# Head norm of a hybrid decoder layer: eight row pieces at a time, or the whole tile with repeated operands

## Chip, cores and metric

One core of a Trainium2 chip runs the whole layer. The metric is device time in microseconds. A profiled execution gives the rows of the trace; its span is counted from the first to the last instruction.

## The reference

One decoder layer on 1024 tokens of width 1024, in float32. Half of the mixing width is multi-scale retention (4 heads of 128), the other half is RWKV-7 time mixing (8 heads of 64). Both read one normalised input projection; their outputs go through one output projection, a SwiGLU feed-forward part and a gated per-layer embedding, and a last RMS norm closes the layer. The part that matters here is the end of the RWKV-7 half, where the output of each head is normalised over its 64 elements:

```python
def head_norm(y, eps):
    mu = jnp.mean(y, axis=-1, keepdims=True)
    var = jnp.mean(jnp.square(y - mu), axis=-1, keepdims=True)
    return (y - mu) * lax.rsqrt(var + eps)

y = head_norm(y, RWKV_GN_EPS).reshape(B, S, W) * ln_w + ln_b
bonus = jnp.sum(r * k * r_k, axis=-1, keepdims=True) * v
return (y + bonus.reshape(B, S, W)) * g
```

## The kernel before

The large products (input projection, output projection, feed-forward) run on TensorE as a stream of 128x512 matmuls. Each float32 weight is loaded, split into a high and a low part (`split`, L249: the high part on ScalarE, the low part at L251 on VectorE or GpSimd), and multiplied in three passes. This stream is the generator `dense`, and its matmuls are the tile `d` of the trace.

The RWKV-7 half is done by `rwkv_group(p, hf)`, once for each pair of heads `p` (four) and each half `hf` of the sequence (two): eight groups. A group goes through the stages prep, ops, A, tok, mid, chain and fin. Stage A holds the inverse of a triangular matrix by 31 steps of two small VectorE operations (L649 to L652, tiles `tmp` and `R`), each of which needs the one before. The inverse of one group runs while an earlier group is in its later stages.

`weave` (L128) gives out the program: it takes a step of the oldest group that may go on, or else a step of a side task (retention, low-rank parts, loads of the mixed output), or else a step of the dense stream. It counts TensorE's estimated time, and each `yield` of a group says how much of it must pass before the next step (FINW, 8049 ns, between the head norm and the transposes behind it, times a factor of 1.58 or 1.98). The order in which an engine finally takes its instructions is planned when the kernel is built, from the order in which they were given out, priorities and estimated costs.

In stage fin the output of a group lies as 128x512 in `Y`, channels down the partitions. TensorE transposes it in four blocks into the PSUM tile `py`, so that tokens lie down the partitions and the row holds eight pieces of 64 elements, one for each head and block. L778 and L779 take mean and variance of each piece into `mv`, L781 the reciprocal root into `rs` (eight values for each partition), both slices of the small tile `fs`. L784 then subtracts the mean and multiplies by the root, one piece at a time, into `yn`. TensorE transposes `yn` back into `pyt`, which takes the same PSUM buffer as `py`, and L789 to L791 apply gain, bias, bonus and gate and write the result out for the output projection.

Of the kernel before, what the change touches and what calls it, by code (L numbers as in the profile page):

```python
# [12 lines left out]
ALU = mybir.AluOpType  # L13
# [3 lines left out]
P = 128  # L17
# [6 lines left out]
C = 64  # L24
# [154 lines left out]
def tile_hybrid_layer(ctx: ExitStack, tc: tile.TileContext, I, out):  # L179
# [3 lines left out]
    V = nc.vector  # L183
# [31 lines left out]
    def K(n):  # L215
        return cst[:, _C[n][0]:_C[n][1]]
# [136 lines left out]
    with ExitStack() as s1:  # L353
# [194 lines left out]
        def v3(t):  # L548
            return t.rearrange("p (u t) -> p u t", t=C)
# [6 lines left out]
        def rwkv_group(p, hf):  # L556
# [9 lines left out]
            def tf(name):  # L566
                return t2.tile([P, HS], F32, tag="f", name=name, bufs=HBUF)
# [63 lines left out]
            for g in range(2):  # L631
# [5 lines left out]
                for j in range(2):  # L637
                    V.tensor_tensor(out=d0v[:, j, us, :], in0=pbv[:, :, 0, j * 32:(j + 1) * 32],
                                    in1=K(f"ms{j}").unsqueeze(1).broadcast_to([P, 4, 32]), op=ALU.mult)
# [5 lines left out]
                            in1=d0v[:, 1].rearrange("p u t -> p t u").unsqueeze(2).broadcast_to([P, 32, 4, NU]), op=ALU.add)  # L645
# [3 lines left out]
            for i in range(31, 0, -1):  # L649
                V.tensor_tensor(out=tmp[:, :, 0:i], in0=Dt[:, i:i + 1, 0:i].broadcast_to([P, 8, i]),  # L650
                                in1=R[:, :, i:i + 1].broadcast_to([P, 8, i]), op=ALU.mult)
# [31 lines left out]
            for src, dst in ((aak, lambda h: XR[:, :, 1, :]), (v3(v), lambda h: Vbd[:, :, h, :]), (bk[:, 0], lambda h: BA[:, :, 0, :]),  # L683
# [5 lines left out]
                for j, h in ((0, 0), (1, 1), (0, 1), (1, 0)):  # L689
# [4 lines left out]
                            in1=K("nblk").unsqueeze(1).unsqueeze(3).broadcast_to([P, NU, 4, 32]), op=ALU.mult)  # L694
# [75 lines left out]
            py = psr.tile([P, 512], F32, tag="rm", name="py")  # L770
# [4 lines left out]
            mv = fs[:, 48:64].rearrange("p (i c) -> p i c", i=8)  # L775
            va, rs, nw = fs[:, 64:72], fs[:, 72:80], fs[:, 80:88]
# [3 lines left out]
            V.tensor_scalar(out=va, in0=mv[:, :, 1], scalar1=64e-5, scalar2=None, op0=ALU.add)  # L780
            rsqrt(rs, va, nw)  # L781
            yn = tf("yn")
            for i in range(8):
                V.tensor_scalar(out=yn[:, i * C:(i + 1) * C], in0=py[:, i * C:(i + 1) * C], scalar1=mv[:, i, 0:1], scalar2=rs[:, i:i + 1], op0=ALU.subtract, op1=ALU.mult)  # L784
            yield "fin", FINW
            pb = psr.tile([P, 512], F32, tag="rm", name="pyt")
            for i in range(4):
# [149 lines left out]
        for o in order:  # L937
            i = int(o[1])
# [363 lines left out]
        for h in range(2):  # L1302
            for k in range(KT):
                tasks[f"mix{h}{k}"] = (mix_load(h, k), 0, ["wo0" if h else "x0free", f"ret{k}{h}" if k < 4 else f"group{k - 4}{h}"])
        weave([(f"group{p}{hf}", rwkv_group(p, hf), need[p]) for hf in range(2) for p in range(4)],
              tasks, dg, count, pe, done)

# [142 lines left out]
    for a, b in passes:  # L1450
        h, n = a // HS, b - a
        t = slice(a - h * HS, b - h * HS)
        for d in range(KT):
# [10 lines left out]
            i = 0  # L1464
# [85 lines left out]
```

## Time and profile before

| | |
|---|---|
| median of 3 runs | 1594.36 us |
| the runs | 1588.4, 1594.36 and 1594.75 us |
| profiled execution | 1588.42 us, its span 1586.6 us |
| mean granted TensorE clock | 0.988 of full speed |
| TensorE busy | 1490.3 us |
| VectorE busy | 1210.2 us |

Busy time of an engine is the time in which at least one of its instructions runs; two that overlap are counted once. PE is TensorE, PEld its weight loads, DVE VectorE, ACT ScalarE and POOL GpSimd.

### The profile page before, as it was taken

How to read it: one execution, taken by the hardware profiler on the slowest of the kernel's cores; microseconds unless marked ns; L12 is line 12 of the kernel's file. 1: busy time of each engine (PE TensorE's matmuls, PEld its weight loads, DVE VectorE, ACT ScalarE, POOL GpSimd, SP SyncE). 2: the span in 40 equal slices, each digit the busy share in tenths (PEclk: the TensorE clock that was granted, in tenths of full speed). 3: DMA queues.
4: the chain of work that ended last, by engine and by line, in shares of the span. 5: the costliest groups of instructions: out<-in, count | busy, mean ns of one | idle time of the engine just before them, and what ended most of it. 6: DMA issues, size and time to landing. Idle time of an engine off the chain costs nothing.

```text
span 1586.6 us, 21684 instructions
## 1 busy us (share of the span) xinstructions
PE 1490.3 (94%) x7328; PEld 1218.7 (77%) x7328; DVE 1210.2 (76%) x2466; ACT 719.9 (45%) x1442; POOL 516.1 (33%) x389
## 2 busy tenths in 40 slices
PE   6999899998988899978889999999999999999997
PEld 5777778786777677767678877778888888888897
DVE  7668896969799878893965545768888888886675
ACT  6655444434535556344344324543333333334554
POOL 7411111111222124324234340545555555570000
PEclk9999999999999999999999999999999999999998
DMA  6544242343634556343243536332223222331222
GB/s 203 173 159 163 96 131 85 102 141 94 197 115 148 185 175 195 93 126 118 84 132 110 179 120 191 117 114 91 89 87 93 90 90 88 119 93 56 84 87 80
DMA packets 108767, 194.09 MB, mean 122 GB/s; under 512 B 12272, under 2 KB 16496, under 8 KB 108656
## 3 DMA queue, kind: packets, MB, share of 16 engines
q1 hardware_dynamic: 108656, 192.71, 38.3%
q8 instruction: 58, 0.95, 0.2%
q14 instruction: 53, 0.43, 0.1%
HBM read 151.24 MB, written 41.42 MB: 121 GB/s over the span
## 4 chain that ended last, share of the span: by engine, by line
PE 63%; DVE 23%; DMA 5%; ACT 4%; issue 3%; POOL 2%; SPq 0%; DVEq 0%; ACTq 0%; POOLq 0%
PE d L190 36%; PE pd L190 14%; PE pg L190 6%; DVE tmp L650 3%; DVE R L652 3%; POOL lo L251 1%; DVE lo L251 1%; DVE Dm L644 1%; DVE inv L603 1%; PE pb L190 1%; DMA st<-in_w_up_dram 1%; DMA st<-in_w_gate_dram 1%; ACT hi L250 1%; PE pq L196 1%; PE pkh L190 1%
## 5 line engine op out<-in xcount | busy, mean ns | idle before, releaser
L190 PE MATMUL d<-hT,hi 128*128 128x512 f32 x1408 | 449.6, 400 | 6.8 <-ACT hi L250 6.8
L251 POOL TENSOR_TENSOR lo<-st,hi 128x512 fp32r<-128x512 f32 x173 | 244.6, 1415 | 571.6 <-ACT hi L250 456.7
L190 PE MATMUL d<-x,hi 128*128 128x512 f32 x960 | 320.4, 409 | 8.3 <-ACT x L339 7.5
L190 PEld LDWEIGHTS d<-hT,hi 128*128 128x128 f32 x1408 | 263.0, 191 | 59.1 <-ACT hi L250 9.2
L190 PE MATMUL d<-hT,lo 128*128 128x512 f32 x704 | 279.6, 397 | 9.8 <-POOL lo L251 4.9
L250 ACT ACTIVATE hi<-st 128x512 fp32r<-128x512 f32 x298 | 186.7, 627 | 222.1 <-PE d L190 70.5
L190 PE MATMUL pd<-ring 128*128 128x512 f32 x948 | 260.4, 389 | 0.0
L190 PEld LDWEIGHTS d<-x,hi 128*128 128x128 f32 x960 | 176.7, 192 | 42.6 <-ACT x L339 7.5
L190 PEld LDWEIGHTS pd<-ring 128*128 128x128 f32 x948 | 178.0, 188 | 37.0
L190 PE MATMUL d<-x,lo 128*128 128x512 f32 x480 | 192.9, 402 | 3.1 <-POOL lo L251 3.1
L190 PEld LDWEIGHTS d<-hT,lo 128*128 128x128 f32 x704 | 134.1, 190 | 42.1 <-DVE lo L251 7.5
L251 DVE TENSOR_TENSOR lo<-st,hi 128x512 fp32r<-128x512 f32 x125 | 117.4, 949 | 51.8 <-ACT hi L250 50.3
L1152 DVE TENSOR_TENSOR x<-x,pd 128x512 f32<-128x512 f32 x180 | 118.5, 679 | 26.9 <-PE pd L190 26.9
L251 POOL TENSOR_TENSOR ring<-xr,ring 128x512 fp32r<-128x512 f32 x53 | 73.4, 1389 | 146.1 <-ACT ring L250 67.1
L250 ACT ACTIVATE ring<-rm 128x512 fp32r<-128x512 f32 x87 | 53.8, 629 | 131.5 <-DVE rm L1085 84.6
L190 PEld LDWEIGHTS d<-x,lo 128*128 128x128 f32 x480 | 91.9, 192 | 23.4 <-POOL lo L251 5.2
L652 DVE TENSOR_TENSOR R<-R,tmp 128x248 f32<-128x248 f32 (+30 forms) x248 | 87.4, 352 | 3.7
L650 DVE TENSOR_TENSOR tmp<-Dt,R 128x248 f32<-128x248 f32 (+30 forms) x248 | 84.2, 339 | 3.4
L190 PE MATMUL d<-mix,hi 128*128 128x512 f32 x256 | 80.7, 395 | 0.9 <-ACT hi L250 0.9
L251 DVE TENSOR_TENSOR ring<-rm,ring 128x512 fp32r<-128x512 f32 x65 | 61.3, 946 | 12.5 <-ACT ring L250 11.6
L250 ACT ACTIVATE ring<-xr 128x512 fp32r<-128x512 f32 x57 | 34.9, 625 | 74.2 <-PE pd L190 73.2
L190 PEld LDWEIGHTS d<-mix,hi 128*128 128x128 f32 x256 | 47.3, 189 | 10.5 <-ACT hi L250 1.3
(315 smaller groups left out, 2389.3 us busy)
## 6 DMA issues: line engine op xcount, KB each, us to landing
st<-in_w_gate_dram SPq DMA_DIRECT2D x88, 256.0 KB, 2.9
st<-in_w_up_dram SPq DMA_DIRECT2D x88, 256.0 KB, 2.9
st<-in_w_in_dram SPq DMA_DIRECT2D x86, 256.0 KB, 2.9
xr<-in_w_down_dram SPq DMA_DIRECT2D x44, 256.0 KB, 2.9
retd<-rt SPq DMA_DIRECT2D x32, 256.0 KB, 2.8
rr<-retd SPq DMA_DIRECT2D x32, 256.0 KB, 3.2
st<-in_w_o_dram SPq DMA_DIRECT2D x32, 256.0 KB, 3.0
rkvd<-rkvt SPq DMA_DIRECT2D x24, 256.0 KB, 2.1
```

Of the source, the lines that this page charges most:

```text
L190: m = nc.tensor.matmul(ps, lhsT, rhs, start=start, stop=stop, skip_group_check=more)
L196: return nc.tensor.transpose(ps, x, ident)
L250: act(hi, src, AF.Copy)
L251: return (eng or V).tensor_tensor(out=lo, in0=src, in1=hi.bitcast(F32), op=ALU.subtract)
L603: V.reciprocal(out=inv, in_=inv)
L644: V.tensor_tensor(out=Dm, in0=d0v[:, 0].rearrange("p u t -> p t u").unsqueeze(2).broadcast_to([P, 32, 4, NU]), in1=d0v[:, 1].rearrange("p ...
L650: V.tensor_tensor(out=tmp[:, :, 0:i], in0=Dt[:, i:i + 1, 0:i].broadcast_to([P, 8, i]), in1=R[:, :, i:i + 1].broadcast_to([P, 8, i]), op=AL ...
L652: V.tensor_tensor(out=R[:, :, 0:i], in0=R[:, :, 0:i], in1=tmp[:, :, 0:i], op=ALU.subtract)
L1152: V.tensor_tensor(out=dst, in0=dst, in1=ps, op=ALU.subtract if name == "P4" else ALU.add)
```

## The change

The eight operations of L784, each on 128x64 with the piece's mean and root as one value for each partition, become two operations on the whole 128x512 tile, seen as 128x8x64. The first subtracts the eight means, the second multiplies by the eight roots in place; mean and root are operands that are repeated along the last axis.

```diff
             yn = tf("yn")
-            for i in range(8):
-                V.tensor_scalar(out=yn[:, i * C:(i + 1) * C], in0=py[:, i * C:(i + 1) * C], scalar1=mv[:, i, 0:1], scalar2=rs[:, i:i + 1], op0=ALU.subtract, op1=ALU.mult)
+            for src, m, op in ((py, mv[:, :, 0:1], ALU.subtract), (yn, rs.unsqueeze(2), ALU.mult)):
+                V.tensor_tensor(out=v3(yn), in0=v3(src), in1=m.broadcast_to([P, 8, C]), op=op)
             yield "fin", FINW
```

`v3` (L548) views a 128x512 tile as 128x8x64.

## Rows read from the trace of the kernel before

**Rows 1.** The page's head: span, and each engine's busy time.
```profile
span 1586.6 us, 21684 instructions
...
PE 1490.3 (94%) x7328; PEld 1218.7 (77%) x7328; DVE 1210.2 (76%) x2466; ACT 719.9 (45%) x1442; POOL 516.1 (33%) x389
```
**Rows 2.** The page's chain that ended last, by engine.
```profile
PE 63%; DVE 23%; DMA 5%; ACT 4%; issue 3%; POOL 2%; SPq 0%; DVEq 0%; ACTq 0%; POOLq 0%
```
**Rows 3.** The changed line's instructions: ns min/median/max, first and last start.
```profile
L784 DVE TENSOR_SCALAR yn<-py,fs x64: 330/339/351, 223.4 to 895.1; 128x64 f32<-128x64 f32 x64
```
**Rows 4.** Chain in order of time, third and sixth group: start us, us, what.
```profile
390.47 0.25 DVE yn L784
...
392.92 0.26 DVE yn L784
...
681.94 0.26 DVE yn L784
...
684.36 0.25 DVE yn L784
```
**Rows 5.** Timeline of VectorE, second group: start us, us, instruction.
```profile
308.97 0.34 DVE L784 TENSOR_SCALAR yn<-py,fs 128x64 f32<-128x64 f32 x1
...
311.67 0.17 DVE L650 TENSOR_TENSOR tmp<-Dt,R 128x8 f32<-128x8 f32 x1
311.75 0.68 DVE L455 TENSOR_TENSOR rt<-d,R 128x512 f32<-128x512 f32 x1
312.35 1.11 DVE L652 TENSOR_TENSOR R<-R,tmp 128x8 f32<-128x8 f32 x1
```
**Rows 6.** Timeline of VectorE, end of the inverse beside the first group.
```profile
227.17 0.18 DVE L650 TENSOR_TENSOR tmp<-Dt,R 128x8 f32<-128x8 f32 x1
227.38 0.18 DVE L652 TENSOR_TENSOR R<-R,tmp 128x8 f32<-128x8 f32 x1
227.59 0.45 DVE L654 STREAM_TRANSPOSE tmp<-R 128x256 f32<-128x256 f32 x1
```
**Rows 7.** Timeline of VectorE, fifth group (eight merged into one row).
```profile
578.18 2.10 DVE L784 TENSOR_SCALAR yn<-py,fs 128x64 f32<-128x64 f32 x8
580.20 0.74 DVE L340 SCALAR_TENSOR_TENSOR hT<-rr,par,hT 128x512 fp32r<-128x512 f32 x1
```
**Rows 8.** Instructions of three lines with two tensor operands, as in rows 3.
```profile
L840 DVE TENSOR_TENSOR rr<-rsc,rmisc x8: 678/682/693, 262.3 to 907.3; 128x512 f32<-128x512 f32 x8
...
L825 DVE TENSOR_TENSOR rr<-rr x16: 628/684/1778, 187.0 to 858.8; 128x512 f32<-128x512 f32 x16
...
L644 DVE TENSOR_TENSOR Dm<-d x8: 2236/2270/2330, 124.0 to 759.4; 128x1024 f32<-128x1024 f32 x8
```
**Rows 9.** Groups of instructions, 200 to 910 us: busy us, mean ns.
```profile
L825 DVE TENSOR_TENSOR rr<-rr 128x512 f32<-128x512 f32 x15 | 12.3, 822 | 0.0
```
**Rows 10.** The page's costliest groups: the two operations of an inverse step.
```profile
L652 DVE TENSOR_TENSOR R<-R,tmp 128x248 f32<-128x248 f32 (+30 forms) x248 | 87.4, 352 | 3.7
L650 DVE TENSOR_TENSOR tmp<-Dt,R 128x248 f32<-128x248 f32 (+30 forms) x248 | 84.2, 339 | 3.4
```
**Rows 11.** Fourth group: the changed line, and the transposes behind it.
```profile
L784 DVE TENSOR_SCALAR yn<-py,fs x8: 336/337/340, 486.3 to 490.6; 128x64 f32<-128x64 f32 x8
...
L196 PEld LDWEIGHTS pyt<-cst,yn x4: 140/140/143, 491.0 to 491.3; 128*128 128x128 f32 x4
```
**Rows 12.** Busy time by stretch: us, then PE, PEld, DVE, ACT, POOL, granted clock, DMA share, GB/s.
```profile
680.00:690.00 10.00, 9.25 (x51) 7.88 (x52) 10.00 (x44) 6.49 (x16) 2.65 (x3) 1.00 0.50 159
...
700.00:710.00 10.00, 6.96 (x35) 5.88 (x35) 8.66 (x10) 5.63 (x16) 1.28 (x1) 0.83 0.74 222
710.00:720.00 10.00, 8.13 (x35) 6.38 (x36) 8.95 (x12) 6.19 (x13) 5.19 (x3) 0.83 0.36 109
720.00:730.00 10.00, 7.90 (x33) 5.59 (x31) 2.08 (x3) 5.27 (x12) 3.53 (x4) 1.00 0.42 131
730.00:740.00 10.00, 9.17 (x33) 7.42 (x34) 2.07 (x3) 2.29 (x4) 3.30 (x3) 0.83 0.43 131
```

## The prediction, made before the change was run

> **What bounds the kernel now.** I read the page's head first, then its chain, then the busy shares by stretch, then the rows of the line that is changed. TensorE is busy 1490.3 of 1586.6 us and VectorE 1210.2 [rows 1], and the chain that ended last runs 63% of the span on TensorE and 23% on VectorE [rows 2]. So a shorter VectorE queue is worth something only where the chain is on VectorE at that moment. The line that is changed runs in eight places, from 223.4 to 895.1 us, once for each pair of heads and each half of the sequence, eight operations each: 64 of them, 339 ns in the median and never outside 330 to 351 ns [rows 3]. What runs after the last of them is untouched, except for the moment at which it starts.
>
> The chain in order of time passes through these operations in two of the eight places: third group, 390.47 to 393.17 us, and sixth group, 681.94 to 684.61 us, each time through all eight [rows 4] (the first and the last of eight). In the other six the chain is on TensorE, ScalarE, GpSimd or a load while they run. That is the first cut: six of eight savings have no direct way to the end of the kernel.
>
> **What is removed.** By busy time the eight operations cost 8 x 0.339 = 2.71 us a group. That is not what they cost the queue. The code gives out the 62 operations of the triangular inverse (L649 to L652) in one piece, yet on the queue they alternate with L784 [rows 5], so the queue's order is planned when the kernel is built. And it is a good fit: the inverse is a chain in which each operation needs the one before it, and an independent operation in between starts before its predecessor has ended. From 308.97 to 311.75 us eight L784 and eight inverse steps go by in 2.78 us [rows 5]. Inverse steps of this width alone stand 0.21 us apart [rows 6], eight take 1.7 us. So the eight L784 lengthen the queue there by 2.78 - 1.7 = 1.1 us, not by 2.71. Six groups (first to fourth, sixth, seventh) alternate like this; in the fifth and eighth the eight stand alone and take 580.20 - 578.18 = 2.02 us [rows 7].
>
> **What is added.** Two operations of 128x512. The first reads PSUM and one small SBUF operand, repeated along the row; its nearest row is L840, PSUM with a repeated SBUF operand, 682 ns with 693 at most [rows 8]. The second reads SBUF twice, in place; nearest is L825, 684 ns in the median but 1778 at most [rows 8] and 822 in the mean over this stretch [rows 9]. A repeated operand as such is free here: L650 has one repeated along the last axis and L652 none, and at equal width they take 339 and 352 ns [rows 10]. The worst stride in the trace is L644, 2270 ns for 1024 elements [rows 8], or 1.14 us for 512; I take 0.68 and keep 1.14 as the bound, since the repeat lies in the operand's last axis as in L650.
>
> In the queue a 512-wide operation between two inverse steps puts them 312.35 - 311.67 = 0.68 us apart instead of 0.21 [rows 5], so it adds 0.47; two add 0.94. An interleaved group thus gains 1.1 - 0.94 = 0.15 us. Alone, the two need 0.68 + 0.03 + 0.60 = 1.31 us (the second waits for the first, the only wait that is added, and the operation queued behind it starts some 0.08 early): gain 2.02 - 1.31 = 0.71 us in the fifth and eighth, where the chain doesn't pass. If other work fills every gap, the eight cost 2.02 and the two 1.20: gain 0.82, the upper end. On the chain the sum is therefore 2 x 0.15 = 0.3 us up to 2 x 0.82 = 1.6 us; the rows with inverse steps between are the nearest, and I take 0.7.
>
> [...]
>
> **The port.** L784 reads PSUM and was not once stretched [rows 3]; the new second operation has two SBUF inputs, the kind that is sometimes stretched to 1.78 us [rows 8]. The mean extra of L825 is 822 - 684 = 0.14 us [rows 9], so 0.28 us in the two places on the chain and 1.1 us in all eight. Taken off the 0.7, the direct effect is -0.4 us. [...]
>
> **What else moves.** The PSUM tile of the transposed heads is freed when its last reader ends: one operation instead of eight, some 2 us sooner. Its next user of note, the transposes back, are put later in TensorE's order by FINW; in the tightest place the last L784 starts at 490.6 and the transposes at 491.0 us [rows 11], right behind other matmuls, so nothing waits there now and nothing is gained. It also shows the thin cover: in the fourth group a second operation stretched by 1.1 us would stand in front of TensorE for about 0.8 us.
>
> **The sum.** Profiled execution: 1588.42 - 0.4 = 1588.0 us. The median of the runs is 5.94 us above the profiled execution (two of the three runs lie there), so the likeliest time is 1594.36 - 0.4, that is 1594.0 us. No change can be told under about 0.5%, 8 us.
>
> **Rivals.**
> *The saving goes through whole (faster).* If VectorE's queue sets the pace in all eight places, the groups give back their busy time: 64 x 0.339 - 16 x 0.685 = 10.7 us, less the mean stretch of 1.1: 1594.4 - 9.6 = 1584.8 us. For it: VectorE is busy all of 680 to 690 us [rows 12], with the chain on it. Against it: the chain touches L784 in two places only, and the interleaving hides over half. With what a shifted plan can give on top I hold this case at 0.26.
>
> *The queue is planned anew for the worse (slower).* Forty-eight operations fewer and sixteen longer ones change the order in which VectorE's ready work is taken, and the long ones cannot be slipped between inverse steps in small change. If a weight split (L251) falls behind, TensorE runs dry. [...] Against it: VectorE is only relieved. Chance 0.16.
>
> *The port takes it back (slower).* Should the second operation meet a GpSimd operation in all eight places, it costs 8 x (1.78 - 0.68) = 8.8 us: 1594.0 + 8.8 = 1602.8 us. It decides only if at least seven of eight collide and each is on the way to the end; the mean of L825 says about two in fifteen (15 x 0.14 / 1.1). Chance 0.06.
>
> **The numbers.** Forecast, within 0.5%: 0.52. Faster 0.26, slower 0.16 + 0.06 = 0.22. The range must hold both the 1584.8 of the one side, with some room for a luckier plan, and the 1601.8 to 1606.9 of the other: 1580 to 1607 us. The forecast's own range is 1586 to 1602.
>
> **What would show it.** In the changed kernel's trace: sixteen operations of about 0.68 us on the changed lines, the first always near 0.68, the second now and then 1.1 to 1.8; VectorE's busy time down by some 10 us while the span hardly moves; inverse steps no longer paired, 0.21 us apart, in the stretch where L784 stood; the chain still on TensorE and loads around 223, 309, 487, 579, 801 and 894 us. I am wrong if the chain leaves VectorE at 390 and 682 us over a microsecond sooner, if TensorE's idle time in 400 to 800 us changes by more than 8 us, or if the order of the splits and loads far from these groups has changed.

## The result: slower by 0.9%, and the profile after

The changed kernel takes 1604.35 us (median of 6 runs, 1597.93 to 1608.65), the kernel before 1588.47 us beside it (6 runs, 1584.71 to 1594.75). The ratio over all runs is 1.0086, with a 95% interval of 1.0069 to 1.0104; the quotient of the two medians, 1.0100, lies within it. I had forecast no change that can be told, with slower at 0.22. The time lies inside the stated range, near its upper end, and that by luck: the upper end was counted from 1594.0 us, where the kernel before has a median of 1588.47, and counted from there it would lie below the time measured.

The page's head of the changed kernel, which answers to [rows 1]:

```profile
span 1603.3 us, 21623 instructions
...
PE 1496.9 (93%) x7328; PEld 1222.3 (76%) x7328; DVE 1204.4 (75%) x2418; ACT 721.0 (45%) x1442; POOL 519.0 (32%) x389
```

VectorE has 48 instructions fewer and is busy 5.8 us less, and the span is 16.7 us longer. TensorE's idle time, the span less its busy time, grows from 96.3 to 106.4 us; the other 6.6 us lie in the busy time of the same 7328 matmuls. So the reader should look for time in which TensorE has nothing to do, and not for a dearer operation on VectorE. The changed line's instructions, the answer to [rows 3], show that there is none:

```profile
L784 DVE TENSOR_TENSOR yn<-py,fs x8: 674/678/683, 220.9 to 906.0; 128x512 f32<-128x512 f32 x8
L784 DVE TENSOR_TENSOR yn<-yn,fs x8: 681/685/691, 225.4 to 910.5; 128x512 f32<-128x512 f32 x8
```

They are sixteen operations of 0.68 us, as sized, and not one of them is stretched in this run. Their last start is 910.5 us where that of the old ones was 895.1 [rows 3]: nearly the whole loss has been made by then. The page's chain by engine, to be held against [rows 2]:

```profile
PE 59%; DVE 23%; DMA 7%; ACT 4%; issue 4%; POOL 2%; SPq 1%; POOLq 0%; ACTq 0%; DVEq 0%
```

TensorE's share falls from 63 to 59%; loads and issue rise by three points together. The chain in order of time, one row from each of five stretches, against [rows 4]:

```profile
220.98 0.59 DVE yn L784
...
392.69 0.59 DVE yn L784
...
492.08 0.59 DVE yn L784
...
693.96 0.59 DVE yn L784
...
809.21 0.59 DVE yn L784
```

Before, the chain passed through the changed line in two of eight places; now it does in five. The new operation that it meets is the first of the pair. That operation needs the means but not the roots, so it is ready earlier than any of the old eight were, and the queue has it there: the timeline of VectorE in the second group, the answer to [rows 5], shows it right behind L780, the first step towards the root.

```profile
306.03 0.16 DVE L780 TENSOR_SCALAR fs<-fs 128x8 f32<-128x8 f32 x1
306.10 0.68 DVE L784 TENSOR_TENSOR yn<-py,fs 128x512 f32<-128x512 f32 x1
...
312.01 0.69 DVE L784 TENSOR_TENSOR yn<-yn,fs 128x512 f32<-128x512 f32 x1
...
314.12 0.75 DVE L789 SCALAR_TENSOR_TENSOR Y<-pyt,par,bv 128x512 f32<-128x512 f32 x1 [0.64 <-PE pyt L196]
314.79 0.98 DVE L652 TENSOR_TENSOR R<-R,tmp 128x24 f32<-128x24 f32 x1
315.69 0.68 DVE L455 TENSOR_TENSOR rt<-d,R 128x512 f32<-128x512 f32 x1
...
316.93 0.68 DVE L679 TENSOR_TENSOR bv<-bo,v 128x512 f32<-128x512 f32 x1
...
319.65 0.43 DVE L654 STREAM_TRANSPOSE tmp<-R 128x256 f32<-128x256 f32 x1
```

The order has changed beyond the two operations. Long ones (L789, L455, L679, L790, L251, L825) now stand between the last steps of the inverse, and the transpose L654 that ends it starts at 319.65 us; before, L679, L790, L251 and L825 stood behind it, and it started at 314.33:

```profile
314.33 0.43 DVE L654 STREAM_TRANSPOSE tmp<-R 128x256 f32<-128x256 f32 x1
```

Set side by side instruction by instruction, the queues that the planner made for the two kernels differ on every engine. To turn one order into the other, 172 of VectorE's instructions have to be moved (the changed line's own not counted), 166 of TensorE's, 74 of ScalarE's, 22 loads and 5 of GpSimd's. All of them lie around six of the eight head norms, the 1st to 4th, the 6th and the 7th. Behind the last of these, at some 840 us, the two kernels have the same order to the end.

### The profile page after: what moved, and what is told of

Same layout as the page of the kernel before. It is cut to its first block, busy times and chain, and to the rows that moved or that the text cites. A ratio compares the mean times of both kernels' runs of the same rounds, so it can differ in the third digit from the quotient of the medians.

```text
span 1603.3 us, 21623 instructions
## 1 busy us (share of the span) xinstructions
PE 1496.9 (93%) x7328; PEld 1222.3 (76%) x7328; DVE 1204.4 (75%) x2418; ACT 721.0 (45%) x1442; POOL 519.0 (32%) x389
## 4 chain that ended last, share of the span: by engine, by line
PE 59%; DVE 23%; DMA 7%; ACT 4%; issue 4%; POOL 2%; SPq 1%; POOLq 0%; ACTq 0%; DVEq 0%
PE d L190 33%; PE pd L190 13%; PE pg L190 6%; DVE R L652 3%; DVE tmp L650 3%; POOL lo L251 2%; DMA st<-mixd 1%; DMA st<-in_w_gate_dram 1%; DVE lo L251 1%; DMA st<-in_w_up_dram 1%; ACT hi L250 1%; DVE Dm L644 1%; DMA rr<-retd 1%; PE pq L196 1%; PE pw L190 1%
## 5 line engine op out<-in xcount | busy, mean ns | idle before, releaser
L251 POOL TENSOR_TENSOR lo<-st,hi 128x512 fp32r<-128x512 f32 x173 | 245.3, 1420 | 575.0 <-ACT hi L250 442.0
L250 ACT ACTIVATE hi<-st 128x512 fp32r<-128x512 f32 x298 | 186.9, 628 | 235.7 <-PE d L190 86.1
L251 DVE TENSOR_TENSOR lo<-st,hi 128x512 fp32r<-128x512 f32 x125 | 114.6, 918 | 56.1 <-ACT hi L250 55.4
L251 POOL TENSOR_TENSOR ring<-xr,ring 128x512 fp32r<-128x512 f32 x53 | 73.3, 1388 | 146.2 <-ACT ring L250 109.7
L250 ACT ACTIVATE ring<-rm 128x512 fp32r<-128x512 f32 x87 | 53.7, 629 | 131.6 <-DVE rm L1085 82.7
L650 DVE TENSOR_TENSOR tmp<-Dt,R 128x248 f32<-128x248 f32 (+30 forms) x248 | 82.6, 333 | 3.3
L251 DVE TENSOR_TENSOR ring<-rm,ring 128x512 fp32r<-128x512 f32 x65 | 59.0, 912 | 12.6 <-ACT ring L250 11.7
L250 ACT ACTIVATE ring<-xr 128x512 fp32r<-128x512 f32 x57 | 34.9, 625 | 74.2 <-PE pd L190 73.2
```

The costliest lines, as they stand in the source:

```text
L250: act(hi, src, AF.Copy)
L251: return (eng or V).tensor_tensor(out=lo, in0=src, in1=hi.bitcast(F32), op=ALU.subtract)
```

## The experiments

**Theory.** The two operations cost nothing measurable; the queues planned anew cost the 0.9%. **Rivals:** the operations themselves cost it (their length between inverse steps, or the port, the author's name for the stretch of an operation beside GpSimd's work; the traces show the stretch, and no run shows a port as its cause), or the inverses alone, which lose their cheap filling and become longer.

To part operations from order, the queue order of one kernel is written into another. The list of positions is stored with the kernel, and each instruction is tied to its predecessor on its own engine by a tie that takes no semaphore. An engine that is held in this way is called pinned here; in the code, positions from 20000 on stand for the operations of the changed line (`fins`), and the numbers 0 to 4 for the queues, 1 being VectorE's.

**The operations in the old order, the old operations in the new order.**

```diff
+    for e, q in enumerate(_queues()):
+        if e in which:
+            row = [plain[t] if t < 20000 else fins[t - 20000] for t in q]
+            for a, b in zip(row, row[1:]):
+                tc.add_manual_dep(b, a.name, info, reason="pin")
...
-        tile_hybrid_layer(tc, aps, out)
+        tile_hybrid_layer(tc, aps, out), pin(tc)
```

The first kernel has the two new operations, the first where the first of the eight stood, the second where the eighth stood.

> The two new operations, with every engine's queue held in the order that the kernel before has: the first operation stands where the first of the eight stood, the second where the eighth stood, all else in its old place. Theory A (the plan of the queues is what costs, the operations do not): the eight inverses together take what they took before, 278 us, and the time is that of the kernel before less 0 to 2 us, so 1586 to 1589 us where the kernel before takes 1588. Rival B (the operations themselves cost: a wait for the port, a wait of the second for the first, TensorE's transposes behind them): the time stays near 1602 to 1605 us although the order is the old one. Rival C (half and half): 1592 to 1600.

Measured: 1592.12 us against 1591.06 of the kernel before beside it, ratio 1.0008 (0.9995 to 1.0021). The second kernel has the eight old operations, all eight where the second new one stands in the changed kernel.

> The eight old operations, with every engine's queue held in the order of the changed kernel: all eight stand one behind the other where the second new operation stands there. Theory A: 1602 to 1607 us, as slow as the changed kernel though none of the new operations is in it, and the eight inverses together take about 293 us. Rival B: back to 1588 to 1592 us, since the old operations are back. Rival C: 1592 to 1600.

Measured: 1606.63 us, 1.0097 (1.0081 to 1.0113). The new order costs the whole loss without one new operation in it, and the new operations cost nothing that can be measured in the old order. The rival of the operations falls.

**VectorE alone in the old order.** New operations, `pin(tc, (1,))`; the other engines are planned freely around it.

> The two new operations, with VectorE's queue alone held in the old order; TensorE, ScalarE, GpSimd and the loads are planned freely. If VectorE's order is the part of the plan that costs (long operations put between the steps of the inverse): 1586 to 1593 us, inverses 278 us. If the order of TensorE and of the loads is what costs, and VectorE's only went along: 1598 to 1606 us.

Measured: 1599.26 us, 1.0054 (1.0036 to 1.0072). The eight inverses, each from its first L650 to L654 and added up, take 276.8 us here, as in the kernel before (278.1), against 293.4 in the changed one; and yet 0.5% is lost. The rival of the inverses explains a part at most.

**The complement:** `pin(tc, (0, 2, 3, 4))`, VectorE free.

> The two new operations, with the orders of TensorE, ScalarE, GpSimd and the loads pinned to those of the kernel before, and VectorE's order left free; the complement of the run with VectorE alone pinned (1.0054). Whole-plan theory (both parts of the new plan cost, VectorE's about 0.3 points and the rest about 0.5): ratio near 1.003, some 1595 to 1597 us beside a kernel before of 1591. Rival, VectorE's own order is what costs and the others only follow: near 1.008, 1604 us. Rival, only agreement of the queues with each other counts, so that any mixture of two plans loses: above 1.005 as in the other mixture.

Measured: 1603.05 us, 1.0074 (1.0055 to 1.0094). Neither half of the old plan saves the time alone. The expected 1.003 was wrong. The rival that VectorE's order is what costs fits this run, but not the run before it; the third case, that queues of two plans don't fit each other and any mixture loses more than 0.5%, fits both, and no run excludes it for the kernel as a whole. The eight inverses take 271.2 us here, less than in the kernel before, and still the run loses 0.74%: the time doesn't go with their length.

**More work in the changed kernel.** The eight old operations are added behind the new ones, writing a tile that is overwritten before anyone reads it.

```diff
+            for i in range(8):
+                V.tensor_scalar(out=Y[:, i * C:(i + 1) * C], in0=py[:, i * C:(i + 1) * C], scalar1=mv[:, i, 0:1], scalar2=rs[:, i:i + 1], op0=ALU.subtract, op1=ALU.mult)
             yield "fin", FINW
```

> The changed kernel with the eight old operations added once more, written into a tile that is dead by then: useless work, 2.7 us of VectorE in each of the eight groups, freely planned. Theory A in its narrow form (the short operations were cheap filling between the steps of the inverse, and without them long ones go in there): the inverses get shorter again, towards 278 us, and the time falls below that of the changed kernel, 1590 to 1598 us, with more work. Theory A in its wide form (any new plan is a new draw): anywhere from 1585 to 1615 us, with the inverses' length going along with the time or not. Rival B (VectorE's work counts): slower than the changed kernel by up to 8 x 2 = 16 us, 1605 to 1620 us.

Measured: 1598.19 us, 1.0046 (1.0029 to 1.0063): faster than the changed kernel with 64 operations more. The inverses take 293.9 us, as long as in the changed one. So more work with another plan takes less time.

**Three other plans.** First, the two new operations kept in program order, so that the first no longer runs ahead of the root.

```diff
-                V.tensor_tensor(out=v3(yn), in0=v3(src), in1=m.broadcast_to([P, 8, C]), op=op)
+                tc.keep_in_program_order(V.tensor_tensor(out=v3(yn), in0=v3(src), in1=m.broadcast_to([P, 8, C]), op=op))
```

> The two new operations, both forced behind the roots in program order, all queues planned freely: a plan that differs from the changed kernel's in a small part. If the first operation's early place (right behind the means, ahead of the root steps) is what spoils the plan: ratio back to 1.000 to 1.003, 1591 to 1596 us. If any new plan costs about the same: 1.006 to 1.011, 1600 to 1608 us.

Measured: 1596.56 us, 1.0032 (1.0012 to 1.0051), between the two cases. That the early place carries a part of the loss isn't shown by it: in the kernel with the eight operations added, and in the one with four operations below, the first operation runs ahead of the root as in the changed kernel, and their 1.0046 and 1.0040 can't be told from 1.0032.

Then nine operations instead of eight, the first head in two halves of 32 columns:

```diff
-            for i in range(8):
+            for i, h in [(i, h) for i in range(8) for h in range(1 + (i == 0))]:
+                w = C // (1 + (i == 0))
...
```

> The kernel before with nine instead of eight operations per group (the first head's as two of 32 columns each), queues planned freely; the work itself grows by some 8 x 0.15 = 1.2 us at most (under 0.001). Whole-plan theory: the time lands away from the kernel before by several tenths of a per cent although the work is the same, ratio 1.004 to 1.012 if the plan of before is a lucky one, and 0.996 to 1.004 if plans scatter on both sides of it. Rival, the new plan of the changed kernel is bad because of what the new operations do to it: ratio 0.999 to 1.002, 1590 to 1594 us.

Measured: 1589.36 us, 0.9983 (0.9971 to 0.9995), with more work and a plan that differs from before by 115 VectorE instructions. At last the change in four operations of 128x256:

```diff
-                V.tensor_tensor(out=v3(yn), in0=v3(src), in1=m.broadcast_to([P, 8, C]), op=op)
+                for i in (0, 4):
+                    V.tensor_tensor(out=v3(yn)[:, i:i + 4], in0=v3(src)[:, i:i + 4], in1=m[:, i:i + 4].broadcast_to([P, 4, C]), op=op)
```

> The change with each of the two operations in two halves of four heads (four operations of 128x256 per group), planned freely: another plan with nearly the same work (some 8 x 0.3 = 2 us more on VectorE). If plans scatter: anywhere from 0.998 to 1.012, and not the 1.0086 of the change. If the wide operations as such do harm to what stands behind them: nearer to before, 1.000 to 1.004. If the cost of the change is one of the early first operation: 1.007 to 1.010, since it is still planned early.

Measured: 1598.91 us, 1.0040 (1.0014 to 1.0065). Kernels whose work differs little and whose plan is their own scatter from 0.9983 to 1.0086: one below the kernel before, and four above it.

**Place by place.** Since the two orders differ in six separate stretches only, each can be taken from either kernel. These four have the new operations throughout and the old order, but for the places named (in code, only the stored list of positions differs). With all six taken from the changed kernel one has that kernel's queues again.

```diff
-QUEUES = '...'   # before's order everywhere
+QUEUES = '...'   # the changed kernel's order around the norms named, before's elsewhere
```

> The new operations; the two plans differ only in a few hundred places that lie around the 1st, 2nd, 3rd, 4th, 6th and 7th head norm, and agree elsewhere. Here the changed kernel's order stands around the 1st and the 3rd norm and the order of before everywhere else. By the lags of the two traces (the changed kernel falls 2.6 us behind at the 1st transpose, is level again at the 2nd, and loses 1.3 us between the 3rd and the 4th) these places cost little: ratio 1.000 to 1.002, 1591 to 1594 us. Rival, every new order costs in proportion to what it moves: about a quarter of 0.86 points, 1.002 to 1.003.

> The changed kernel's order around the 2nd head norm alone, the order of before elsewhere. By the lags (0.6 us behind at the 2nd transpose, 9.4 us at the 3rd) this is the dearest place: plus 6 to 9 us, ratio 1.004 to 1.006, 1597 to 1600 us. Rival, a local loss is caught up by what stands ready later, and only the sum of many places shows: 1.000 to 1.002.

> The changed kernel's order around the 4th head norm alone (the place where it moves most instructions), the order of before elsewhere. By the lags (10.7 us at the 4th transpose, 16.3 us at the 5th): plus 4 to 6 us, ratio 1.0025 to 1.004, 1595 to 1597 us. Rival, loss in proportion to what is moved: this place has the most, plus 5 to 7 us and the dearest of the four. Rival, caught up later: 1.000 to 1.002.

> The changed kernel's order around the 6th and 7th head norm, the order of before elsewhere. By the lags (17.3 us at the 6th transpose, 13.1 us at the 7th, 16.7 us at the 8th and at the end): between minus 1 and plus 2 us, ratio 0.999 to 1.002, 1590 to 1594 us. Rival, loss in proportion to what is moved: plus 3 to 4 us, 1.002 to 1.003. If the four runs of this call add up to 1.007 to 1.010, the cost is a sum of places; if each is near 1.000, it comes from their meeting.

| order of the changed kernel around | us | ratio to before (95%) |
|---|---|---|
| 1st and 3rd norm | 1595.86 | 1.0020 (1.0008 to 1.0033) |
| 2nd norm | 1597.23 | 1.0036 (1.0021 to 1.0050) |
| 4th norm | 1596.79 | 1.0031 (1.0016 to 1.0046) |
| 6th and 7th norm | 1592.40 | 1.0010 (0.9998 to 1.0022) |

The excesses add up to 0.97%. Each holds the 0.08% of the pinned kernel without any such place, so above it they are 0.12 + 0.28 + 0.23 + 0.02 = 0.65%, and with the 0.08 once, 0.73%: within the interval of the changed kernel's 0.86. The cost is about the sum of local losses. The 2nd norm, where VectorE's order moves little (14 instructions), costs no less, as far as can be told, than the 4th (81): the cost isn't in proportion to what moves. By the lags (how far the changed kernel is behind the one before at each norm, read from the two traces) the 2nd norm had been expected at 1.004 to 1.006; 1.0036 is somewhat less, and the rival that a local loss is caught up later (1.000 to 1.002) falls for this norm.

**The 2nd norm by queue.** VectorE's order there alone from the changed kernel, and then the other four queues' alone (again only the stored list).

> The new operations; around the 2nd head norm VectorE alone in the changed kernel's order (long operations between the last inverse steps), every other queue and every other place in the order of before. In the run with the whole place, the last step of the inverse ended 2.3 us later, the reciprocal began 2.5 us later, the L612 product 3.5 us and ScalarE's hbd 4.2 us later, and TensorE waited 2.8 us for it. Theory, VectorE's order carries the loss: plus 3 to 5 us, ratio 1.002 to 1.0035. Rival, ScalarE's conversion put ahead of hbd and the loads' order carry it: under 1.001.

> The complement: around the 2nd head norm TensorE, ScalarE, GpSimd and the loads in the changed kernel's order, VectorE in that of before. Theory, VectorE's order carries the loss: ratio 1.000 to 1.0015. Rival, the other queues carry it: 1.002 to 1.0035. Third case, the queues must fit each other: this and the complement both at 1.002 or above.

Measured: VectorE alone 1599.53 us, 1.0042 (1.0027 to 1.0058); the others alone 1592.47 us, 1.0000 (0.9985 to 1.0016). At this place it is VectorE's order, and the case that queues of two plans don't fit each other falls here. How 14 moved instructions cost 4 to 5 us above the kernel with the new operations in the old order can be followed in three timelines of this stretch. First the new operations in the old order, VectorE and then ScalarE and TensorE:

```profile
315.37 0.43 DVE L654 STREAM_TRANSPOSE tmp<-R 128x256 f32<-128x256 f32 x1
315.73 0.65 DVE L679 TENSOR_TENSOR bv<-bo,v 128x512 f32<-128x512 f32 x1
...
316.61 0.74 DVE L790 SCALAR_TENSOR_TENSOR Y<-Y,par,sg 128x512 f32<-128x512 f32 x1
...
319.79 0.69 DVE L251 TENSOR_TENSOR hs<-kk,hs 128x512 fp32r<-128x512 f32 x1
...
322.46 0.67 DVE L825 TENSOR_TENSOR rr<-rr 128x512 f32<-128x512 f32 x1
...
324.31 3.35 DVE L603 RECIPROCAL inv<-inv 128x512 f32<-128x512 f32 x1
...
330.59 0.68 DVE L612 TENSOR_TENSOR bk<-inv,en 128x512 f32<-128x512 f32 x1
...
333.87 1.11 ACT L712 ACTIVATE hbd<-psm 32x128 f32<-32x128 f32 x4
...
336.14 0.97 PE L190 MATMUL psm<-Xd,hbd 128*128 128x32 f32 x8
```

The same instructions with the 2nd place in the changed kernel's order, all queues:

```profile
312.12 0.75 DVE L789 SCALAR_TENSOR_TENSOR Y<-pyt,par,bv 128x512 f32<-128x512 f32 x1 [0.65 <-PE pyt L196]
...
314.94 0.68 DVE L679 TENSOR_TENSOR bv<-bo,v 128x512 f32<-128x512 f32 x1
...
315.62 0.74 DVE L790 SCALAR_TENSOR_TENSOR Y<-Y,par,sg 128x512 f32<-128x512 f32 x1
...
316.36 0.68 DVE L251 TENSOR_TENSOR hs<-kk,hs 128x512 fp32r<-128x512 f32 x1
...
317.05 0.68 DVE L825 TENSOR_TENSOR rr<-rr 128x512 f32<-128x512 f32 x1
317.65 0.43 DVE L654 STREAM_TRANSPOSE tmp<-R 128x256 f32<-128x256 f32 x1
...
326.77 3.34 DVE L603 RECIPROCAL inv<-inv 128x512 f32<-128x512 f32 x1
...
331.77 1.77 DVE L610 SCALAR_TENSOR_TENSOR inv<-k,par,inv 128x512 f32<-128x512 f32 x1
...
334.07 0.68 DVE L612 TENSOR_TENSOR bk<-inv,en 128x512 f32<-128x512 f32 x1
...
338.02 1.11 ACT L712 ACTIVATE hbd<-psm 32x128 f32<-32x128 f32 x4
...
339.18 1.08 PE L190 MATMUL psm<-Xd,hbd 128*128 128x32 f32 x8 [2.83 <-ACT hbd L712]
```

And with VectorE's order alone:

```profile
314.80 0.75 DVE L789 SCALAR_TENSOR_TENSOR Y<-pyt,par,bv 128x512 f32<-128x512 f32 x1 [1.92 <-PE pyt L196]
...
319.40 0.43 DVE L654 STREAM_TRANSPOSE tmp<-R 128x256 f32<-128x256 f32 x1
...
328.98 3.34 DVE L603 RECIPROCAL inv<-inv 128x512 f32<-128x512 f32 x1
...
336.34 0.68 DVE L612 TENSOR_TENSOR bk<-inv,en 128x512 f32<-128x512 f32 x1
...
339.62 1.11 ACT L712 ACTIVATE hbd<-psm 32x128 f32<-32x128 f32 x4
...
340.78 1.92 PE L190 MATMUL psm<-Xd,hbd 128*128 128x32 f32 x8 [4.41 <-ACT hbd L712]
```

The reader is to see a delay that grows down the queue. L789, which needs the transposes back from TensorE, has been put among the last inverse steps, waits 0.65 us, and everything behind it waits with it. The larger part comes from four long operations, L679, L790, L251 and L825: in the old order they stand behind the transpose L654 that ends the inverse, in the changed one in front of it, and there they take 2.5 us. The inverse ends 2.28 us later (317.65 - 315.37), the reciprocal of 3.35 us begins 2.46 us later, L612 3.48 us later (L610 is stretched to 1.77 us), ScalarE comes to hbd 4.15 us later (a split of 0.63 us, L250, has been put in front of it there), and TensorE, which waited for nothing there in the old order, stands still for 2.83 us. With the old TensorE order around it the transposes come later still, L789 waits 1.92 us, and TensorE's wait is 4.41 us. The windows from 330 to 350 us of the first of the three kernels (us, then PE, PEld, DVE, ACT, POOL, granted clock, DMA share, GB/s):

```profile
330.00:340.00 10.00, 10.00 (x54) 8.54 (x53) 6.06 (x10) 5.93 (x14) 3.89 (x3) 1.00 0.61 200
340.00:350.00 10.00, 10.00 (x62) 8.83 (x60) 1.64 (x4) 3.02 (x8) 0.43 (x1) 1.00 0.32 109
```

and of the third:

```profile
330.00:340.00 10.00, 6.37 (x32) 5.04 (x31) 9.49 (x11) 3.70 (x7) 1.67 (x3) 0.94 0.55 182
340.00:350.00 10.00, 9.22 (x39) 7.92 (x40) 0.69 (x1) 4.55 (x13) 2.56 (x2) 0.72 0.55 166
```

TensorE loses 3.63 + 0.78 us, and in the slice behind the wait its mean granted clock is 0.72 in place of 1.00.

**The new operations in the plan of the nine.** All queues in the order of the kernel with nine operations; the second new operation stands where the last of the nine stood.

```diff
-QUEUES = '...'   # before's order
+QUEUES = '...'   # the order planned for nine operations a group
```

> The two new operations with all queues pinned to the order that was planned for the kernel with nine operations per group (0.9983), the second new operation where the last of the nine stood. If the time goes with the order and not with the operations: 0.997 to 1.000, 1587 to 1591 us beside 1591, which would beat both kernels or equal the one before. Rival, 0.9983 was the edge of the scatter: 1.000 to 1.002.

Measured: 1589.85 us against 1591.60, 0.9983 (0.9971 to 0.9994), the very ratio of the nine in that order. The time goes with the order here as well, and not with the length of the inverses, which take 282.8 us, more than in the kernel before. This version beats both kernels, the one before by 0.17%, which is less than the 0.5% below which the prediction counted times as the same.

## Why the prediction was wrong, step by step

- **What is removed and added: right in its terms, as far as can be measured.** The operations take 678 and 685 ns where 0.68 was taken. In the old order one of them puts two inverse steps 0.72 us apart (309.90 to 310.62 us in the second group), against the 0.68 that I read from [rows 5]. The direct effect of -0.4 us fits 1.0008 (0.9995 to 1.0021, or -0.8 to +3.3 us), and with one order for both, nine operations and two come out alike (0.9983). VectorE's busy time was to fall by some 10 us and fell by 5.8, and by 6.6 with the old order: the 10.7 was a sum of durations, and busy time counts overlap once. An L784 of the kernel before overlaps its successor by 0.08 us (308.97 + 0.34 us [rows 5], against 309.23 for the inverse step behind it), which for 48 operations is 3.8 us of the sum, by estimate.
- **The port: right as a stretch that happens, and without effect here.** In the kernel before, three of L825's sixteen are stretched, each beside an operation of GpSimd's that had begun before it: 1.73 us from 186.96 beside L251 from 186.87 to 188.15, 1.77 us from 631.83 beside L824 from 631.33 to 633.06, and 1.78 us from 858.84 beside L251 from 858.60 to 860.07. Each ends 0.54 or 0.55 us behind GpSimd's operation; why, no run shows. Another, at 629.59 us beside L251 from 629.48 to 631.35, took only 0.63 us. In the changed kernel the second operation was never stretched (691 ns at most); in two experiments one of eight was, to 1477 and 1643 ns (rows below). That is two of the 40 second operations of five runs (the changed kernel, the new operations in the old order, in nine's order, and the 2nd norm with all queues and with VectorE alone), below the two in fifteen that I took from L825. The rival that it takes the gain back didn't occur.
- **"Six of eight savings have no direct way to the end": true of the old plan only.** In the new one the chain meets the changed line in five places.
- **The sum is the step that failed.** "Profiled execution: 1588.42 - 0.4" takes the order of all queues as given, although the part on what is removed says that this order is planned when the kernel is built. The term put at nothing is the new plan: +0.97% with the old operations in it, some 15 us, against 0.4 us of direct effect. The base was off too: the sum was set on the median of three runs, 1594.36, and the six lie at 1588.47, where the profiled execution of 1588.42 had been.
- **The rival "planned anew for the worse" was the right case, with too small a chance.** Its 1601.8 to 1606.9 us hold the 1604.35 measured, but by luck: counted from its own base of 1594.0 it is a loss of 7.8 to 12.9 us, and the 0.86% are 13.7. That loss was sized by 700 to 740 us of the kernel before: 7.8 us in which TensorE is idle, and, by estimate, 5.1 us for three slices at a granted clock of 0.83 [rows 12]. No run shows that a new plan brings one more such stretch; in the changed kernel TensorE's idle time is 10.1 us longer, and its busy time 6.6 us. The rival's mechanism was half right: TensorE runs dry and its granted clock falls (at the 2nd norm, with VectorE's order alone, a wait of 4.41 us and a clock of 0.72 in the slice behind it), but not for want of a weight split in one stretch as long as that of [rows 12]. Four sets of places cost 0.02 to 0.28% each above the kernel with the new operations in the old order, and at the 2nd norm, the one place that was followed, the wait is for hbd, behind a late inverse. "VectorE is only relieved" was no argument against it: the time isn't monotone in the work, as 64 operations more in the changed kernel show (1.0046 instead of 1.0086).
- **The signs of being wrong were too coarse.** TensorE's idle time from 400 to 800 us, which was to change by more than 8 us, went from 45.3 to 48.0; the largest growth, 4.1 us, lies from 200 to 400 us. And no order far from the groups has changed. What did fail is the chain, which was to stay on TensorE and loads around 223, 487 and 801 us and is on the changed line there.
- **The PSUM tile freed sooner** was counted at nothing; no run tests that alone.

What stays open: which queues make the loss at the 4th norm, how the loss arises at the other places, and why the run with only VectorE pinned still loses 0.54%. The planner's own reason for its new order wasn't looked into either, and that the first new operation needs no root is not shown to matter.

## What to carry to other kernels

Where the order of the queues is planned from the instructions, an edit has two prices, its own and that of the new plan, and for an edit of a few us the second can be the larger: here nothing that can be measured against 0.9%, with plans of nearly the same work 1% apart. Give a forecast a term for it, of either sign, and before an edit is judged, run its instructions in the old order and the old instructions in its order. An operation that can start before the others is no gain by itself; look at what then stands in front of the chain that other engines wait for, and fix the order once it is good.

## What the runs showed of the hardware

Small operations too were stretched beside GpSimd's work. In the changed kernel an inverse operation of 128x24 took 0.98 us from 314.79 (timeline above), where the one of that width before it took 0.18 us and GpSimd, in the timeline of its own, was at work:

```profile
314.45 1.27 POOL L251 TENSOR_TENSOR lo<-st,hi 128x512 fp32r<-128x512 f32 x1 [21.32 <-DMA rr<-retd]
```

The operation ends at 315.77, 0.05 us behind the end of GpSimd's. Here small steps were no shelter: one collision cost 0.8 us in the inverse, more than a new operation takes. It is no cost of the change, though: in the kernel before, an inverse operation of 128x8 takes 1.11 us in the same stretch [rows 5] and ends at 313.46, 0.02 us behind a GpSimd operation that ran from 312.15 to 313.44. The second new operation in the run with nine's order, and in the one with VectorE alone at the 2nd norm, by its longest duration:

```profile
L784 DVE TENSOR_TENSOR yn<-yn,fs x8: 648/684/1477, 227.2 to 897.1; 128x512 f32<-128x512 f32 x8
```

```profile
L784 DVE TENSOR_TENSOR yn<-yn,fs x8: 683/686/1643, 227.6 to 903.9; 128x512 f32<-128x512 f32 x8
```

The first of them is from one of the two fastest kernels of the study, so that one such stretch need not show in the time.
